# Weight sums of the first feed-forward unit: the second adding DMA writes to DRAM, onto a plain copy of the block, and the transfers of this stage keep program order

## The chip, the cores and the metric

One core of one Trainium2 chip runs the whole program. The metric is the device time of one execution in microseconds (us). The kernel before takes 1514.77 us, the median of three runs (1513.19 to 1515.32). One further execution was profiled; all rows below are from it.

## The reference

The kernel computes one transformer block on 528 tokens (16 meta tokens and 512 real ones) with a model width of 1024, all in float32: a gated feed-forward unit of width 2816, a mixer with retention and sparse attention, a second feed-forward unit, and norms between them.

```python
def swiglu(u, w_gate, w_up, w_down):
    return (jax.nn.silu(u @ w_gate) * (u @ w_up)) @ w_down
...
h = h + 0.5 * swiglu(rmsnorm(h, ffn1_norm[l]), ffn1_w_gate[l], ffn1_w_up[l], ffn1_w_down[l])
h = h + hybrid_mixer(rmsnorm(h, mix_norm[l]), ...)
h = h + 0.5 * swiglu(rmsnorm(h, ffn2_norm[l]), ffn2_w_gate[l], ffn2_w_up[l], ffn2_w_down[l])
y = rmsnorm(h, final_norm)
```

The change concerns the first `swiglu` alone.

## The kernel before

**Products.** Each float32 operand is split in a high and a low part (`whi`, `wlo`: ScalarE makes the high one, VectorE the low one), and each product is made of three TensorE passes. To save passes, blocks of 2 x 2 are multiplied with seven products in place of eight, which needs sums and differences of blocks on both sides.

**Gate and up.** The 22 column tiles of the hidden layer are taken in pairs; `f` is the first tile of a pair. A pair takes eight steps on TensorE: four for the gate weights (one "seven", lines 448 to 515), then four for the up weights. The four steps hold 2, 2, 2 and 1 of the seven products. One load brings the weights of a seven, 1024 KB, into one of two buffers `raw`. It is issued by SyncE (SP) in line 133. A load is written in the program four steps ahead of the step that uses it, and the sums of weights for a seven (lines 466, 467, 471 on VectorE) are made while the seven before it is at its second and third step. So VectorE reads a load about two steps before TensorE does, and a buffer is free once VectorE has made the low part of its last quarter.

**The spill.** For the 16 tiles from `F0` = 4 to `F1` = 20, eight pairs counted by `k`, the product silu(gate) * up is not multiplied with the down weights at once. It goes to DRAM (`hx1`) with four sums of its token and tile halves: `spill1` makes the sums on VectorE (lines 915 to 917, tile `ts`) and stores them with three DMAs from GpSimd (POOL), lines 918 and 920.

**The weight sums.** The down weights of the same 16 tiles are needed in sums of blocks too. For each `k` there are four blocks of 128 x 512 (256 KB). Line 929 loads the left and the right block of the first row, the right one twice (`first`, `total`, `other`). An adding DMA of POOL adds the right block of the second row onto `total` (line 931). `sums1` makes two differences on VectorE (lines 936 and 937), stores three results to DRAM (`wx1`, lines 938 to 940, by SP), lets a second adding DMA add the left block of the second row onto `first` in SBUF (line 941, POOL), and stores that sum from POOL (line 942).

**Where this is called.** `s1.extra` is a list of functions. One is taken off in the first step of each seven and one in the fourth. For pair `k` these are `nothing`, `nothing`, `sums1` (first step of the up seven) and `bring_next` (fourth step of the up seven), which calls `bring1` for `k` + 1. `bring1(0)` is called ahead of the pipeline.

**Order.** TensorE, VectorE and ScalarE run in the order in which the code is written. The DMA issues on SP and POOL are placed by a scheduler, which may move one ahead of another that was written before it, except where `keep_in_program_order` pins it. Before, only the DMAs of the products after this stage are pinned (`in_order`). A queue issues in order: an issue that waits holds back all that stand behind it on the same engine. Where the code of `R` and `wq` speaks of buffers: `first` alternates between `wq` and one of the two `R`, `total` takes the other `R`, and `other` has the single `ssum2`. All R and ssum2 tiles are named `hraw` in the rows.

Of the kernel before, what the change touches and what calls it, by code (L numbers as in the profile page):

```python
# [11 lines left out]
F32 = mybir.dt.float32  # L12
F32R = mybir.dt.float32r
AF = mybir.ActivationFunctionType
ALU = mybir.AluOpType
# [3 lines left out]
P = 128  # L19
D = 1024  # L20
KD = D // P
S = 512
# [59 lines left out]
def kernel(ctx: ExitStack, tc: tile.TileContext, x, meta, g1, wg1, wu1, wd1, gm,  # L82
                      w_in, w_ro, w_ao, w_mo, g2, wg2, wu2, wd2, gf, rope, decay, causal, out):
    nc = tc.nc
# [173 lines left out]
    R = cpool.tile([P, T], F32, name="R", tag="R", bufs=2)  # L258
    late = {}
    ssum2 = cpool.tile([P, T], F32, name="ssum2", tag="ssum2")  # L260
# [11 lines left out]
    hx1 = dpool.tile([8, P, 8, TH], F32, name="hx1")  # L272
# [71 lines left out]
    class Sevens:  # L344
# [103 lines left out]
        def seven(self, src_w, f, take, soon=False):  # L448

            d, th = {}, self.th  # L450
            c1, c2 = slice(0, P), slice(P, 2 * P)

            def product(ps, w, j, name, first):
                mm3([(ps[:, :th], slice(0, th))], [t[:, j : j + 4, :] for t in w], self.moving(name), 4, first, True, not first)

            def copy(name, ps):
                d[name] = self.rooms.tile([P, th], F32, tag=name, name=name, bufs=2)
                nc.scalar.activation(d[name], ps[:, :th], AF.Copy)

            def pre1():  # L460
                d["raw"] = load_w(src_w[:, f * P : (f + 2) * P], KD, 2 * P)

            def pre2():
                raw = d["raw"]
                s = d["s"] = self.wsum()[:, : 16 * P].rearrange("p (a k c) -> p a k c", a=4, k=4)
                nc.vector.tensor_tensor(s[:, 1], raw[:, :4, c2], raw[:, 4:, c2], ALU.add)
                nc.vector.tensor_tensor(s[:, 0], s[:, 1], raw[:, :4, c1], ALU.subtract)

            def pre3():
                raw, s = d["raw"], d["s"]  # L470
                nc.vector.tensor_tensor(s[:, 2], raw[:, :4, c1], raw[:, :4, c2], ALU.subtract)
                self.sum4 = lambda: nc.vector.tensor_tensor(s[:, 3], raw[:, 4:, c1], s[:, 0], ALU.subtract)

            def run1(w, lower):
                d["X"], d["Z"], d["Y"] = (self.bank(f"psq{c}") for c in "XZY")
                product(d["X"], w, 0, "B11", True)
                copy("p1", d["X"])
                lower()
                product(d["Z"], w, 4, "B21", True)
                take(0, d["Z"], d["p1"])  # L480
                self.catch_up()
                if self.extra:
                    self.extra.pop(0)()

            def run2(w, lower):
                product(d["X"], w, 0, "T2", False)
                copy("u2", d["X"])
                lower()
                product(d["Y"], w, 4, "T1", True)
                copy("p5", d["Y"])  # L490

            def run3(w, lower):
                product(d["X"], w, 0, "T3", False)
                take(3, d["X"], d["p5"])
                lower()
                self.next_sum4()
                product(d["Y"], w, 4, "B22", False)
                take(1, d["Y"], d["u2"])

            def run4(w, lower):  # L500
                product(d["X"], w, 0, "T4", False)
                if not soon:
                    lower()
                take(2, d["X"], None)
                if soon:
                    lower()
                if self.extra:
                    self.extra.pop(0)()

            return [(pre1, lambda: d["raw"][:, :, c1], run1),  # L510
                    (pre2, lambda: d["s"][:, 0:2].rearrange("p a k c -> p (a k) c"), run2),
                    (pre3, lambda: d["s"][:, 2:4].rearrange("p a k c -> p (a k) c"), run3),
                    (lambda: None, lambda: d["raw"][:, 4:, c2], run4)]

# [55 lines left out]
    if True:  # L570
# [335 lines left out]
        def one_row(tag):  # L906

            return cpool.tile([P, T], F32, tag=tag, name="hraw", bufs=2 if tag == "R" else 1)

        def spill1(f, u):  # L910

            k = (f - F0) // 2
            all4 = hidp.tile([P, 2, TX], F32, tag=turn(room_tags), name="ts")[:, :, :T].rearrange("p a (b t) -> p a b t", b=2)
            ts = [all4[:, i // 2, i % 2] for i in range(4)]
            nc.vector.tensor_tensor(all4[:, :, 0], u[:, 1::2], u[:, 0:2], ALU.subtract)
            nc.vector.tensor_tensor(ts[1], ts[0], u[:, 3], ALU.subtract)
            nc.vector.tensor_tensor(ts[3], u[:, 2], ts[1], ALU.add)
            nc.gpsimd.dma_start(hx1[0:4, :, k, :].rearrange("o p t -> p o t"), u)
            for i in range(2):
                nc.gpsimd.dma_start(hx1[4 + 2 * i : 6 + 2 * i, :, k, :].rearrange("o p t -> p o t"), all4[:, i])  # L920

        blocks = {}

        def bring1(k):

            blocks["now"] = []
            for tag, (half, cs) in zip((("wq", "R")[k % 2], "R", "ssum2"), ((0, C1), (0, C2), (0, C2))):
                t = hidp.tile([P, S], F32, tag="wq", name="wq") if tag == "wq" else one_row(tag)[:, :S]
                nc.sync.dma_start(t, wrows1[half][:, k, cs])
                blocks["now"].append(t)  # L930
            nc.gpsimd.dma_start(blocks["now"][1], wrows1[1][:, k, C2], accum_op=ALU.add)

        def sums1(k):

            first, total, other = blocks["now"]
            nc.vector.tensor_tensor(other, first, other, ALU.subtract)
            nc.vector.tensor_tensor(first, first, total, ALU.subtract)
            nc.sync.dma_start(wx1[1, :, k, :], other)
            nc.sync.dma_start(wx1[0, :, k, :], total)
            nc.sync.dma_start(wx1[2, :, k, :], first)  # L940
            nc.gpsimd.dma_start(first, wrows1[1][:, k, C1], accum_op=ALU.add)
            nc.gpsimd.dma_start(wx1[3, :, k, :], first)

        def nothing(k):
            pass

        def bring_next(k):

            if k < 7:
                bring1(k + 1)  # L950

        s1.spill = {f: (lambda u, f=f: s1.behind.append(lambda: spill1(f, u))) for f in range(F0, F1, 2)}
        s1.extra = [lambda k=k, do=do: do(k) for k in range(8) for do in (nothing, nothing, sums1, bring_next)]
        unit, ahead, streams = {}, [4], {}

        def in_order(*args):

            tc.keep_in_program_order(nc.sync.dma_start(*args))

        def load_row(src, nk, n):  # L960

# [281 lines left out]
        class Values:  # L1243
# [63 lines left out]
            def take(self, bank_, r):  # L1307
                v = self.by_columns(r)
                nc.vector.tensor_tensor(v, self.by_tokens(self.d[bank_ + "w"]), v, ALU.add)
# [78 lines left out]
        steps += units[1].steps(units[2], rope_beside(ret_k, slice(0, T))) + [gate_step(OFF_GR + P, 1)]  # L1388
        steps += units[2].steps(None, rope_beside(ret_q, REAL))
        n_dense = len(steps)  # L1390
        bring1(0)
        pipe = steps_through(steps, ahead)
        with tc.manual_schedule(engines=BUSY):
            pr = s1.spare("l", "pr")
# [1299 lines left out]
```

## Time and profile before

| | |
|---|---|
| median of three runs | 1514.77 us |
| the profiled execution: its own time | 1514.32 us |
| its span, first to last instruction | 1512.4 us |
| TensorE busy | 99% of the span |
| VectorE busy | 78% of the span |
| the stage of the eight spilled pairs | about 85 to 266 us of the span |
| mean DMA rate over the span | 171 GB/s |

The profile has one row for each group, wait or instruction. Rows of engines are named PE (TensorE), PEld (its weight loads), DVE (VectorE), ACT (ScalarE), POOL (GpSimd), and SPq for the DMA issues of SyncE. The row of a DMA shows when it was issued; "to landing" is the time from there until its data had arrived. Idle time stands in square brackets behind an instruction, with what ended it.

### The profile page before, as it was taken

The page shows a single profiled execution, that of the slowest core. Times are in us where ns is not written, and L with a number is a line of the kernel's source. Part 1 is how long each engine was busy: PE and PEld are TensorE (multiplying, and loading weights), DVE is VectorE, ACT ScalarE, POOL GpSimd, SP SyncE. Part 2 cuts the span into 40 slices and gives each one's busy share as a digit, 9 for nine tenths or more (in the row PEclk, how much of TensorE's full clock was granted, in tenths as well). Part 3 has the DMA queues.
Part 4 walks back from the last instruction along what each step waited for, and adds up shares of the span by engine and source line. Part 5 has one row for each costly group of instructions (what it writes and reads, how often), then busy time and mean ns, then how long its engine had stood idle before and what let it go on. Part 6 is the DMA issues. An engine that isn't in the chain of part 4 may idle for free.

```text
span 1512.4 us, 24591 instructions
## 1 busy us (share of the span) xinstructions
PE 1496.7 (99%) x9647; PEld 1351.6 (89%) x9647; DVE 1179.3 (78%) x1820; ACT 752.2 (50%) x1204; POOL 190.1 (13%) x237
## 2 busy tenths in 40 slices
PE   9999999999999999999999999999999999999998
PEld 8999999999988888788898889999888889999986
DVE  4998898789787767677968676777575788999877
ACT  5655455567354444542333455555335345555555
POOL 1011121001111111000000021111002003222101
PEclk9999999999999999999999999999999999999999
DMA  5259887886645435232322485456583223455693
GB/s 183 85 168 269 242 245 238 292 283 199 236 139 177 168 133 170 87 98 87 108 97 85 99 208 164 149 180 204 166 271 112 84 84 124 163 175 174 232 321 136
DMA packets 183235, 258.44 MB, mean 171 GB/s; under 512 B 9360, under 2 KB 120616, under 8 KB 182224
## 3 DMA queue, kind: packets, MB, share of 16 engines
q1 hardware_dynamic: 164784, 207.42, 42.4%
q0 software_dynamic: 15088, 43.63, 10.1%
q10 hardware_dynamic: 3248, 5.84, 1.2%
q8 instruction: 75, 1.23, 0.3%
q14 instruction: 40, 0.33, 0.1%
HBM read 204.40 MB, written 49.82 MB: 168 GB/s over the span
## 4 chain that ended last, share of the span: by engine, by line
PE 88%; DVE 6%; DMA 4%; issue 1%; ACT 0%; DVEq 0%; ACTq 0%
PE psqX L157 8%; PE psrg L157 6%; PE psro L157 6%; PE psvX L1335 4%; PE psqY L157 4%; DMA raw<-in_ffn_w_gate_dram 3%; PE psrk L157 3%; PE psak L157 3%; PE psu L157 3%; PE psrq L157 3%; PE psgate L157 3%; PE psmo L157 3%; PE psga L157 3%; PE psaq L157 3%; PE psat L157 3%; PE psX L1010 2%
## 5 line engine op out<-in xcount | busy, mean ns | idle before, releaser
L292 DVE TENSOR_TENSOR wlo<-raw,whi 128x1024 fp32r<-128x1024 f32 (+2 forms) x205 | 224.3, 1095 | 47.8 <-ACT whi L291 47.0
L291 ACT ACTIVATE whi<-raw 128x1024 fp32r<-128x1024 f32 (+2 forms) x205 | 192.6, 941 | 129.8 <-PE psqZ L157 21.3
L157 PE MATMUL psqX<-th,whi 128*128 128x264 f32 (+1 forms) x432 | 124.5, 288 | 7.2 <-DVE g L538 5.1
L157 PE MATMUL psqX<-tl,whi 128*128 128x264 f32 (+1 forms) x432 | 122.6, 284 | 0.0
L157 PE MATMUL psqX<-th,wlo 128*128 128x264 f32 (+1 forms) x432 | 122.5, 284 | 0.0
L117 ACT ACTIVATE whi<-raw 128x1024 fp32r<-128x1024 f32 (+1 forms) x58 | 60.3, 1043 | 85.9 <-issue 18.4
L118 DVE TENSOR_TENSOR wlo<-raw,whi 128x1024 fp32r<-128x1024 f32 (+1 forms) x58 | 69.9, 1205 | 40.0 <-ACT whi L117 39.9
L291 ACT ACTIVATE whi<-wsum 128x1024 fp32r<-128x1024 f32 x72 | 76.1, 1057 | 38.6 <-issue 12.6
L157 PEld LDWEIGHTS psqX<-th,whi 128*128 128x128 f32 x432 | 82.2, 190 | 9.6 <-DVE g L538 6.1
L292 DVE TENSOR_TENSOR wlo<-wsum,whi 128x1024 fp32r<-128x1024 f32 x72 | 86.4, 1217 | 0.8 <-ACT whi L291 0.7
L157 PEld LDWEIGHTS psqX<-th,wlo 128*128 128x128 f32 x432 | 82.4, 191 | 0.0
L157 PEld LDWEIGHTS psqX<-tl,whi 128*128 128x128 f32 x432 | 82.3, 191 | 0.0
L157 PE MATMUL psro<-vo,whi 128*128 128x512 f32 x256 | 79.3, 391 | 0.0
L157 PEld LDWEIGHTS psro<-vo,whi 128*128 128x128 f32 x256 | 48.1, 188 | 10.5 <-ACT whi L291 0.2
L157 PE MATMUL psrg<-xh,whi 128*128 128x512 f32 x128 | 51.8, 405 | 0.0
L157 PE MATMUL psro<-vo,wlo 128*128 128x512 f32 x128 | 50.3, 393 | 0.0
L157 PE MATMUL psrg<-xh,wlo 128*128 128x512 f32 x128 | 50.0, 391 | 0.0
L157 PE MATMUL psrg<-xl,whi 128*128 128x512 f32 x128 | 50.0, 390 | 0.0
L292 DVE TENSOR_TENSOR wlo<-w,whi 128x1024 fp32r<-128x1024 f32 x30 | 36.5, 1222 | 13.1 <-ACT whi L291 13.1
L2488 POOL TENSOR_TENSOR ts<-g 128x256 f32<-128x256 f32 x16 | 22.3, 1410 | 176.8 <-DVE g L549 96.3
L291 ACT ACTIVATE whi<-w 128x1024 fp32r<-128x1024 f32 x30 | 31.7, 1057 | 20.1 <-PE psvX L1335 10.9
L157 PE MATMUL psqX<-xh,whi 128*128 128x264 f32 (+1 forms) x144 | 41.3, 286 | 0.0
(516 smaller groups left out, 4832.6 us busy)
## 6 DMA issues: line engine op xcount, KB each, us to landing
raw<-in_ffn_w_up_dram SPq DMA_DIRECT2D x22, 1024.0 KB, 5.2
raw<-in_ffn_w_gate_dram SPq DMA_DIRECT2D x21, 1024.0 KB, 7.1
raw<-in_w_in_dram SPq DMA_DIRECT2D x19, 1024.0 KB, 5.1
raw<-in_ffn_w_down_dram SPq DMA_DIRECT2D x34, 512.0 KB, 4.6
raw<-wx SPq DMA_DIRECT2D x32, 512.0 KB, 5.6
raw<-in_w_in_dram SPq DMA_DIRECT2D x31, 512.0 KB, 4.1
w<-in_w_in_dram SPq DMA_DIRECT2D x24, 512.0 KB, 6.6
wq<-in_ffn_w_down_dram SPq DMA_DIRECT2D x36, 256.0 KB, 5.2
```

The lines of the kernel that those rows point to most:

```text
L117: nc.scalar.activation(hi, src, AF.Copy)
L118: eng.tensor_tensor(lo, src, hi.bitcast(F32), ALU.subtract)
L157: nc.tensor.matmul(o, a[:, k, :], b[:, sl], start=first and k == 0 and i == 0, stop=last and k == nk - 1 and i == 2, skip_group_check=onto)
L291: nc.scalar.activation(hi, src, AF.Copy)
L292: return lambda: nc.vector.tensor_tensor(lo, src, hi.bitcast(F32), ALU.subtract)
L1010: nc.tensor.matmul(pss[c], a[:, k, c * P : (c + 1) * P], m[:, k, :], start=first and k == 0 and i == 0, stop=last and k == 1 and i == 2, s ...
L1335: nc.tensor.matmul(d[bank_][t], a, b[:, k, :], start=not onto and j + k + m == 0, stop=j + k == 3 and m == 2, skip_group_check=onto)
L2488: nc.gpsimd.tensor_tensor(ts[:, i], a, b, ALU.subtract)
```

## The change

The second adding DMA no longer adds onto `first` in SBUF. The left block of the second row of weights is copied from DRAM to DRAM, into its place in `wx1`, ahead of time; the adding DMA then adds `first` from SBUF onto that place, and the store that followed goes. `first` always has the buffer `wq`, is loaded by POOL and not by SP, and is brought in the first step of the next gate seven. `bring_next` moves from the fourth step of the up seven to the third. All DMAs of the weight sums and of the spill are pinned to program order. `spill1` runs in `catch_up`, ahead of the function taken from `s1.extra`, so the three stores to `hx1` stand on POOL ahead of the load of `first`. The order of instructions on TensorE and ScalarE is the same as before; on VectorE it is the same too, only that in four of the eight pairs `first` lies in `wq` in place of `hraw`.

```diff
@@ run3 and run4 of a seven
                 product(d["Y"], w, 4, "B22", False)
                 take(1, d["Y"], d["u2"])
+                if self.extra:
+                    self.extra.pop(0)()
...
                 if soon:
                     lower()
-                if self.extra:
-                    self.extra.pop(0)()
@@ spill1
-            nc.gpsimd.dma_start(hx1[0:4, :, k, :].rearrange("o p t -> p o t"), u)
+            pool_order(hx1[0:4, :, k, :].rearrange("o p t -> p o t"), u)
             for i in range(2):
-                nc.gpsimd.dma_start(hx1[4 + 2 * i : 6 + 2 * i, :, k, :].rearrange("o p t -> p o t"), all4[:, i])
+                pool_order(hx1[4 + 2 * i : 6 + 2 * i, :, k, :].rearrange("o p t -> p o t"), all4[:, i])
@@ weight sums
-        def bring1(k):
-
-            blocks["now"] = []
-            for tag, (half, cs) in zip((("wq", "R")[k % 2], "R", "ssum2"), ((0, C1), (0, C2), (0, C2))):
-                t = hidp.tile([P, S], F32, tag="wq", name="wq") if tag == "wq" else one_row(tag)[:, :S]
-                nc.sync.dma_start(t, wrows1[half][:, k, cs])
-                blocks["now"].append(t)
-            nc.gpsimd.dma_start(blocks["now"][1], wrows1[1][:, k, C2], accum_op=ALU.add)
+        def in_order(*args):
+
+            tc.keep_in_program_order(nc.sync.dma_start(*args))
+
+        def pool_order(*args, **how):
+
+            tc.keep_in_program_order(nc.gpsimd.dma_start(*args, **how))
+
+        def bring_two(k):
+
+            total, other = one_row("R")[:, :S], one_row("ssum2")[:, :S]
+            for t in (total, other):
+                in_order(t, wrows1[0][:, k, C2])
+            pool_order(total, wrows1[1][:, k, C2], accum_op=ALU.add)
+            return [total, other]
+
+        def bring_first(k):
+
+            t = hidp.tile([P, S], F32, tag="wq", name="wq")
+            pool_order(t, wrows1[0][:, k, C1])
+            return [t]
 
         def sums1(k):
 
-            first, total, other = blocks["now"]
+            total, other, first = blocks["now"]
             nc.vector.tensor_tensor(other, first, other, ALU.subtract)
             nc.vector.tensor_tensor(first, first, total, ALU.subtract)
-            nc.sync.dma_start(wx1[1, :, k, :], other)
-            nc.sync.dma_start(wx1[0, :, k, :], total)
-            nc.sync.dma_start(wx1[2, :, k, :], first)
-            nc.gpsimd.dma_start(first, wrows1[1][:, k, C1], accum_op=ALU.add)
-            nc.gpsimd.dma_start(wx1[3, :, k, :], first)
+            for i, t in ((1, other), (0, total), (2, first)):
+                in_order(wx1[i, :, k, :], t)
+            pool_order(wx1[3, :, k, :], first, accum_op=ALU.add)
+
+        def bring_next(k):
+
+            blocks["now"] = bring_two(k + 1)
+            pool_order(wx1[3, :, k + 1, :], wrows1[1][:, k + 1, C1])
+
+        def next_first(k):
+
+            if k:
+                blocks["now"] += bring_first(k)
...
-        s1.extra = [lambda k=k, do=do: do(k) for k in range(8) for do in (nothing, nothing, sums1, bring_next)]
+        s1.extra = [lambda k=k, do=do: do(k) for k in range(8) for do in (next_first, nothing, sums1, bring_next)][:31]
@@ ahead of the pipeline
-        bring1(0)
+        blocks["now"] = bring_two(0) + bring_first(0)
+        pool_order(wx1[3, :, 0, :], wrows1[1][:, 0, C1])
```

The order on SP, before, over one pair and a half. `raw` is a load of gate or up weights, `wx_92` is `wx1`; L929 loads blocks of the down weights, L938 to L940 store `other`, `total` and `first`.

```order
L940 DMA wx_92<-wq 128x512
L929 DMA hraw<-in_ffn_w_down_dram 128x512 x2
L133 DMA raw<-in_ffn_w_up_dram 128x8x256
L939 DMA wx_92<-hraw 128x512
L929 DMA wq<-in_ffn_w_down_dram 128x512
L133 DMA raw<-in_ffn_w_gate_dram 128x8x256
L938 DMA wx_92<-hraw 128x512
L940 DMA wx_92<-hraw 128x512
L929 DMA hraw<-in_ffn_w_down_dram 128x512 x2
L133 DMA raw<-in_ffn_w_up_dram 128x8x256
```

The same place on SP in the changed program, where all pinned DMAs have the line of their helper, L926.

```order
L926 DMA wx_92<-wq 128x512
L926 DMA hraw<-in_ffn_w_down_dram 128x512 x2
L133 DMA raw<-in_ffn_w_up_dram 128x8x256
L133 DMA raw<-in_ffn_w_gate_dram 128x8x256
L926 DMA wx_92<-hraw 128x512 x2
L926 DMA wx_92<-wq 128x512
L926 DMA hraw<-in_ffn_w_down_dram 128x512 x2
L133 DMA raw<-in_ffn_w_up_dram 128x8x256
```

Between the load of the up weights and that of the next gate weights stood the store of `total`, which waits for its adding DMA, and the load of `first`. Both have left this place: the store stands behind the gate load, with the two others, and the load is POOL's.

The order on POOL before, over one pair and a half: the second adding DMA (L941), the first one (L931), the store of the sum (L942), the three stores of the spill (L918, L920).

```order
L941 DMA wq<-in_ffn_w_down_dram 128x512
L931 DMA hraw<-in_ffn_w_down_dram 128x512
L942 DMA wx_92<-wq 128x512
L918 DMA hx_91<-g 128x4x264
L920 DMA hx_91<-ts 128x2x264 x2
L941 DMA hraw<-in_ffn_w_down_dram 128x512
L931 DMA hraw<-in_ffn_w_down_dram 128x512
L942 DMA wx_92<-hraw 128x512
```

The same place on POOL in the changed program, where the helper's line is L930.

```order
L930 DMA wx_92<-wq 128x512
L930 DMA hraw<-in_ffn_w_down_dram 128x512
L930 DMA wx_92<-in_ffn_w_down_dram 128x512
L930 DMA hx_91<-g 128x4x264
L930 DMA hx_91<-ts 128x2x264 x2
L930 DMA wq<-in_ffn_w_down_dram 128x512
L930 DMA wx_92<-wq 128x512
L930 DMA hraw<-in_ffn_w_down_dram 128x512
```

The store that waited for the second adding DMA and stood ahead of the spill is gone; a copy from DRAM to DRAM stands there, which waits for no result of this pair. Behind the spill follows the load of `first`, and then the adding DMA onto DRAM, which is the first row.

More of the change, by code (lines that the diff above doesn't have):

```diff
@@ L942, in sums1 @@
-            nc.gpsimd.dma_start(wx1[3, :, k, :], first)
+            for i, t in ((1, other), (0, total), (2, first)):
[7 more added lines that the diff above has]
+                blocks["now"] += bring_first(k)
         def nothing(k):
             pass
-        def bring_next(k):
-            if k < 7:
-                bring1(k + 1)
@@ L952 @@
         s1.spill = {f: (lambda u, f=f: s1.behind.append(lambda: spill1(f, u))) for f in range(F0, F1, 2)}
-        s1.extra = [lambda k=k, do=do: do(k) for k in range(8) for do in (nothing, nothing, sums1, bring_next)]
+        s1.extra = [lambda k=k, do=do: do(k) for k in range(8) for do in (next_first, nothing, sums1, bring_next)][:31]
         unit, ahead, streams = {}, [4], {}
-        def in_order(*args):
-            tc.keep_in_program_order(nc.sync.dma_start(*args))
         def load_row(src, nk, n):
```

## The prediction

> **What bounds the kernel now.** TensorE is the bound nearly everywhere, so I first ask how much it loses at all. The page's head gives the span and the busy time.
>
> ```profile
> span 1512.4 us, 24591 instructions
> PE 1496.7 (99%) x9647; PEld 1351.6 (89%) x9647; DVE 1179.3 (78%) x1820; ACT 752.2 (50%) x1204; POOL 190.1 (13%) x237
> ```
>
> TensorE is idle for only 15.7 us. The second view, busy time by stretches of the span, shows where; the numbers are the stretch, its length, busy PE, PEld, DVE, ACT and POOL, the granted clock, the DMA share and GB/s.
>
> ```profile
> 30.00:120.00 90.00, 90.00 (x748) 89.83 (x747) 79.34 (x119) 49.90 (x79) 6.82 (x8) 1.00 0.48 143
> 120.00:180.00 60.00, 56.32 (x458) 55.16 (x456) 52.12 (x78) 29.71 (x47) 13.68 (x18) 1.00 0.89 261
> 180.00:190.00 10.00, 9.87 (x69) 9.87 (x70) 8.05 (x13) 5.45 (x10) 0.00 (x0) 0.83 0.65 206
> 190.00:210.00 20.00, 20.00 (x169) 20.00 (x167) 17.50 (x26) 10.90 (x18) 4.56 (x6) 1.00 0.91 265
> 210.00:250.00 40.00, 36.69 (x300) 36.04 (x299) 35.74 (x53) 20.14 (x31) 9.17 (x12) 1.00 0.85 244
> 250.00:300.00 50.00, 50.00 (x415) 49.91 (x414) 40.82 (x58) 28.33 (x44) 3.65 (x5) 1.00 0.81 270
> ```
>
> The stage of the change loses 3.68 + 0.13 + 3.31 = 7.1 us of TensorE, and once the clock falls: 0.83 over 10 us is another 1.7 us. Ahead of it and behind it nothing is lost. So **8.8 us is all that this stage can give**, 0.6% of the span. The third view, the waits from 90 to 280 us, says who ends the idle time (total, times, longest).
>
> ```profile
> DVE wsum L466 <- DMA raw<-in_ffn_w_gate_dram: 10.3, 6, 3.1
> DVE wsum L466 <- DMA raw<-in_ffn_w_up_dram: 2.1, 1, 2.1
> PE psqX L157 <- DVE g L538: 5.1, 5, 2.1
> PE psqX L157 <- DVE g L524: 2.0, 1, 2.0
> ```
>
> TensorE waits for VectorE, and VectorE for a load: 10.3 us for gate weights, 2.1 us for up weights. Those 12.4 us cost 8.8 us of TensorE, 0.71 us for each. The gate loads come too late. Why, is read from the timeline of the pair at 100 to 124 us: SP (with the last up load, seven pairs on), then POOL, then VectorE.
>
> ```profile
> 102.29 0.38 SPq L133 DMA_DIRECT2D raw<-in_ffn_w_up_dram  x1
> 111.74 0.33 SPq L939 DMA_DIRECT2D wx<-hraw  x1
> 113.51 0.33 SPq L929 DMA_DIRECT2D wq<-in_ffn_w_down_dram  x1
> 113.94 1.06 SPq L133 DMA_DIRECT2D raw<-in_ffn_w_gate_dram  x1
> ...
> 255.76 0.38 SPq L133 DMA_DIRECT2D raw<-in_ffn_w_up_dram  x1
> ```
>
> ```profile
> 103.40 0.90 POOL L941 DMA_DIRECT2D wq<-in_ffn_w_down_dram  x1 [61.68 <-DVE g L538]
> 105.32 0.86 POOL L931 DMA_DIRECT2D hraw<-in_ffn_w_down_dram  x1 [1.02 <-DMA hraw<-in_ffn_w_down_dram]
> 110.76 0.58 POOL L942 DMA_DIRECT2D wx<-wq  x1 [4.58 <-DMA wq<-in_ffn_w_down_dram]
> 111.33 0.81 POOL L918 DMA_DIRECT2D hx<-g  x1
> 112.12 1.43 POOL L920 DMA_DIRECT2D hx<-ts  x2
> ```
>
> ```profile
> 106.48 1.25 DVE L549 TENSOR_TENSOR g<-g,st 128x1056 f32<-128x1056 f32 x1
> 110.33 0.43 DVE L917 TENSOR_TENSOR ts<-g,ts 128x264 f32<-128x264 f32 x1
> 110.68 0.69 DVE L466 TENSOR_TENSOR wsum<-raw 128x512 f32<-128x512 f32 x1
> 112.01 0.68 DVE L292 TENSOR_TENSOR wlo<-raw,whi 128x512 fp32r<-128x512 f32 x1
> 119.85 0.69 DVE L937 TENSOR_TENSOR hraw<-hraw 128x512 f32<-128x512 f32 x1
> 122.16 0.69 DVE L466 TENSOR_TENSOR wsum<-raw 128x512 f32<-128x512 f32 x1 [1.61 <-DMA raw<-in_ffn_w_gate_dram]
> ```
>
> The gate load's buffer is free at 112.69, when the last low part is made. VectorE asks for the data at 120.54. That leaves 7.85 us. SP issues at 113.94, since the store L939 (waiting for the adding DMA) and the load of `first` stand ahead; the load takes 8.2 us and is 1.6 us late. Two causes, then: 1.25 us of queueing at most, and a slow transfer. The next rows show why it is slow: first the busy share of the DMA engines in four stretches of this pair, then issue to landing from 100 to 266 us.
>
> ```profile
> 102.00:104.00 2.00, 2.00 (x19) 2.00 (x19) 1.95 (x4) 0.75 (x1) 0.60 (x1) 1.00 0.68 138
> 104.00:111.00 7.00, 7.00 (x61) 7.00 (x60) 6.93 (x11) 3.82 (x6) 1.39 (x3) 1.00 1.02 260
> 111.00:112.00 1.00, 1.00 (x11) 1.00 (x10) 0.96 (x2) 0.48 (x2) 1.00 (x2) 1.00 0.14 47
> 112.00:122.00 10.00, 10.00 (x85) 10.00 (x84) 7.79 (x12) 6.01 (x10) 1.54 (x3) 1.00 1.00 326
> ```
>
> ```profile
> raw<-in_ffn_w_up_dram SPq DMA_DIRECT2D x8, 1024.0 KB, 5.6
> raw<-in_ffn_w_gate_dram SPq DMA_DIRECT2D x7, 1024.0 KB, 8.2
> wx<-hraw SPq DMA_DIRECT2D x18, 256.0 KB, 2.9
> hraw<-in_ffn_w_down_dram SPq DMA_DIRECT2D x17, 256.0 KB, 3.9
> hx<-g POOLq DMA_DIRECT2D x8, 528.0 KB, 4.5
> hx<-ts POOLq DMA_DIRECT2D x16, 264.0 KB, 5.7
> wq<-in_ffn_w_down_dram POOLq DMA_DIRECT2D x4, 256.0 KB, 7.1
> wx<-wq POOLq DMA_DIRECT2D x4, 256.0 KB, 2.5
> ```
>
> From 112 to 122 the DMA engines are full (1.00, 326 GB/s). Just before, at 111, they stand nearly empty (0.14): POOL waited 4.58 us for its adding DMA, and with it waited the three spill stores, 1056 KB, whose first data had been ready since 107.73. Then the spill, the store L942, the load of `first` and the gate load fall into one stretch.
>
> **The change, part by part.** *Gate load on SP.* It now stands right behind the up load, so it is issued when its buffer is free: 1.25 us earlier here. Nothing waits longer for it. *Spill stores on POOL.* Line 918 needs only the product that is ready at 107.73, and POOL is then through with the adding DMA of `total` (105.32) and the copy (about 106.2 to 107). So 528 KB leave at 107.8 in place of 111.33, and the two others at 110.76, when L917 ends, in place of 112.12. *Other transfers.* The store of `total` (L939) moves behind the gate load, to 119.9; the store L942 goes. Out of the gate load's stretch fall 528 KB + 256 KB + 256 KB, 1.06 MB, or 3.3 us at 326 GB/s. The gate load lands at about 122.1 - 3.3 = 118.8 in place of 122.1, before 120.54, with 1.7 us to spare. **The 10.3 us of gate waits go: 10.3 x 0.71 = 7.3 us.** VectorE has no instruction more, so nothing new is late there.
>
> *Up load.* What left the gate stretch arrives here. The store of `total` now lies ahead of the up load on SP (256 KB, 0.8 us at 326 GB/s), and the adding DMA L941 no longer waits for the store of `first`, so it lands more within the up load. There is room: 0.32 x 2 = 0.6 us unused from 102 to 104 and 0.86 us from 111 to 112. The up load came in time at 110.68, where L466 shows no wait. The copy and the early spill store are issued behind it, from 106 on. I let the one up wait of 2.1 us stay, 1.5 us of TensorE.
>
> *The pinned loads of `total` and `other`* are issued at the same place as before, right behind the stores; `bring_next` comes one step earlier only in the program. Their buffers are the same, so the cost is nothing; what would show otherwise is a wait of SP ahead of them.
>
> *The load of `first`* now follows the spill on POOL: issued at about 110.76 + 1.43 = 112.2, needed before L936 at about 119.1. From below, the store L942 (2.5 us) has it there at 114.7; from above, POOL's adding load from the same weights (7.1 us) at 119.3, 0.2 us late. Without the reading of a destination I take 5.7, as for `hx<-ts`: 117.9. Cover gone, each us costs VectorE a us and TensorE 0.71.
>
> *Adding onto DRAM, and the copy.* No row shows either. For the adding DMA the bounds are a plain store (2.5 us) and an adding load plus another reading of DRAM (7.1 + 3.9 = 11.0 us); I take 7.1, the nearest row, since it too reads and writes 256 KB once each. The copy lies between 2.5 and 3.9 + 2.5 = 6.4 us; I take 3.9. Neither is waited for by an engine: `first`'s buffer must be free by 112.2, and issued at about 103.4 the sum has 8.8 us for that. Against a load, a store and an adding DMA before, the number of 256 KB transfers is unchanged at nine per pair, and they may even cost less than before.
>
> The TensorE clock: the fall to 0.83 stands right behind an idle time of 2.0 us, and the sum counts it as lost through waits. The Trainium skill ("TensorE: Matmul & The Clock Gate", Part 1) puts the fall to half speed behind an idle window of about 3.4 us; the longest wait here is 2.1 us, so by that rule these waits would not explain it, and 1.7 us of the gain would be uncertain.
>
> **Sum.** The profiled execution took 1514.3 us (span 1512.4 and 1.9 around it), 0.5 us below the median of the runs, 1514.77. 1514.3 - 8.8 + 1.5 = **1507.0 us**.
>
> **Rivals.** *The engines are full, and the wait only moves to the up load.* For it: shares of 0.89 and 0.91 over long stretches, the up load's thin margin, 1.02 from 104 to 111. Against it: the hole at 111. With waits of 1.5 to 2 us at each of eight up loads VectorE waits 12 to 16 us again; at 0.71 that is 8.5 to 11.4 us, so 1514 to 1517. The Trainium skill ("DMA: Bandwidth & Descriptors", Issuing engines are not separate DMA queues) speaks for this: issuing from another engine only saves issue time, since all transfers share the same 16 engines. The row at 111 agrees only in part, because there the order left the engines idle. Chance 0.14.
>
> *`first` is late.* POOL issues it 7 us before it is needed. If it lands 9 us after its issue, VectorE waits 2 us in seven pairs, 14 x 0.71 = 10 us, about 1515; if 8 us, about 1511. Against it: half of the spill is gone from the engines by then. Chance 0.10.
>
> *Slower: adding onto DRAM holds the DMA engines.* A pair moves 2 x 1024 + 9 x 256 + 1056 = 5408 KB, 5.54 MB. At 261 GB/s for a share of 0.89, full engines need 18.9 us for that. A pair now lasts (255.76 - 102.29) / 7 = 21.9 us; without loss, (153.5 - 8.8) / 7 = 20.7. If one 256 KB sum onto DRAM occupies the engines 1.8 us longer than the sum in SBUF, the gain begins to go; above 3.0 us a pair is longer than now. At 4.0 us longer each of eight pairs loses 1.0 us against now: 1522. Chance 0.13.
>
> *The gate loads issue no earlier* because something else holds SP. The order on SP excludes it, but for the wait on the buffer itself.
>
> **How the numbers follow.** The forecast, waits mostly gone, has 0.63 and reaches from 1504.5 (all 8.8 us and run to run noise) to 1511. A change within 0.2%, 3 us, can't be told from none in this kernel. Adding the first two rivals up to 1517 leaves out only the slower case and a little: **1504.5 to 1517**. Faster 0.66 (a part of the late `first` is still faster), the same 0.20, slower 0.14.
>
> **What would show it.** Right: gate loads land in 5 to 6.5 us and VectorE's waits on them vanish; POOL issues the store of `g` within 1 us of L549's end; TensorE's idle time from 120 to 250 us falls below 2 us; no clock below 1.00 at 180 us. Wrong: waits of L466 on up loads, or of L936 on `wq`, or a landing of the adding DMA onto DRAM above 10 us with a share near 1.00 throughout.

## The result, and the profile after

The changed kernel takes 1504.84 us, the median of six runs (1503.93 to 1505.61); the kernel before, on the same chip, 1515.05 (1512.02 to 1516.67). The ratio is 0.9935 with a 95% interval of 0.9922 to 0.9948: 0.65% faster, inside the range and 2.2 us below the predicted 1507.0. The execution that was profiled took 1505.61 us.

The page's head, the changed kernel:

```profile
span 1503.8 us, 24586 instructions
PE 1493.6 (99%) x9647; PEld 1349.3 (90%) x9647; DVE 1179.7 (78%) x1820; ACT 752.2 (50%) x1204; POOL 194.3 (13%) x245
```

The span is 8.6 us shorter. TensorE's idle time fell from 15.7 to 1503.8 - 1493.6 = 10.2 us, and its busy time by 3.1 us, for the same 9647 matmuls; by the estimate of the prediction 1.7 us of that are the clock. Where the idle time went, the view by stretches shows (columns as before):

```profile
120.00:180.00 60.00, 59.04 (x489) 58.73 (x488) 55.98 (x83) 32.23 (x51) 15.36 (x21) 1.00 0.90 273
180.00:190.00 10.00, 10.00 (x85) 10.00 (x84) 9.46 (x14) 5.85 (x11) 1.12 (x2) 1.00 0.77 214
190.00:210.00 20.00, 19.57 (x163) 19.36 (x162) 18.40 (x28) 10.39 (x18) 5.15 (x8) 1.00 0.89 265
210.00:250.00 40.00, 40.00 (x335) 40.00 (x334) 38.08 (x57) 22.12 (x36) 9.96 (x14) 1.00 0.90 273
```

The stage now loses 0.96 + 0.43 = 1.4 us in place of 7.1, and the clock stays at 1.00 from 180 to 190. VectorE's waits for loads and TensorE's waits for VectorE in the changed kernel, from 90 to 280 us (total, times, longest):

```profile
DVE wsum L466 <- DMA raw<-in_ffn_w_gate_dram: 2.0, 2, 1.9
DVE wsum L466 <- DMA raw<-in_ffn_w_up_dram: 1.1, 2, 0.8
PE psqX L157 <- DVE g L538: 1.0, 1, 1.0
PE psqX L157 <- DVE g L524: 0.4, 1, 0.4
```

VectorE waits 3.1 us for weights, where it waited 12.4. No row has VectorE waiting for `first`. Why the loads are in time, the timelines of the changed kernel show: SP, then POOL, in the pair that was shown of before.

```profile
102.64 0.38 SPq L133 DMA_DIRECT2D raw<-in_ffn_w_up_dram  x1
113.07 0.38 SPq L133 DMA_DIRECT2D raw<-in_ffn_w_gate_dram  x1
```

```profile
100.98 0.90 POOL L930 DMA_DIRECT2D wx<-wq  x1 [57.17 <-DVE wq L950]
106.37 0.87 POOL L930 DMA_DIRECT2D hraw<-in_ffn_w_down_dram  x1 [4.49 <-DMA hraw<-in_ffn_w_down_dram]
106.92 0.87 POOL L930 DMA_DIRECT2D wx<-in_ffn_w_down_dram  x1
108.38 0.82 POOL L930 DMA_DIRECT2D hx<-g  x1 [0.59 <-DVE g L549]
110.94 1.43 POOL L930 DMA_DIRECT2D hx<-ts  x2 [1.74 <-DVE ts L916]
112.37 0.55 POOL L930 DMA_DIRECT2D wq<-in_ffn_w_down_dram  x1
```

Between the up load and the gate load SP issues nothing. POOL issues the store of `g` at 108.38 (before: 111.33), right after the 0.59 us that it waits for the data itself, and the two stores of `ts` at 110.94 (before: 112.12). The busy share of the DMA engines in the same four stretches:

```profile
102.00:104.00 2.00, 2.00 (x19) 2.00 (x18) 1.95 (x5) 1.10 (x2) 0.00 (x0) 1.00 1.06 234
104.00:111.00 7.00, 7.00 (x61) 7.00 (x60) 6.93 (x10) 3.82 (x6) 2.30 (x4) 1.00 1.02 282
111.00:112.00 1.00, 1.00 (x10) 1.00 (x10) 0.97 (x3) 0.13 (x1) 1.00 (x2) 1.00 1.08 387
112.00:122.00 10.00, 10.00 (x85) 10.00 (x84) 9.22 (x14) 6.02 (x11) 1.73 (x3) 1.00 0.76 265
```

The hole at 111 (0.14) is filled, and the gate load's stretch from 112 to 122 has fallen from 1.00 to 0.76. From issue to landing, 100 to 266 us:

```profile
raw<-in_ffn_w_up_dram SPq DMA_DIRECT2D x8, 1024.0 KB, 8.1
raw<-in_ffn_w_gate_dram SPq DMA_DIRECT2D x7, 1024.0 KB, 6.8
wx<-wq POOLq DMA_DIRECT2D x8, 256.0 KB, 6.1
wx<-in_ffn_w_down_dram POOLq DMA_DIRECT2D x7, 256.0 KB, 5.6
wq<-in_ffn_w_down_dram POOLq DMA_DIRECT2D x7, 256.0 KB, 4.7
```

The gate load takes 6.8 us in place of 8.2, the up load 8.1 in place of 5.6: traffic has moved from the one to the other, as the prediction had it, and the up load is late by only 1.1 us in all.

### The profile page after: what moved, and what is told of

It reads as the page before. It is cut to its first block, busy times and chain, and to the rows that moved or that the text cites. A ratio compares the mean times of both kernels' runs of the same rounds, so it can differ in the third digit from the quotient of the medians.

```text
span 1503.8 us, 24586 instructions
## 1 busy us (share of the span) xinstructions
PE 1493.6 (99%) x9647; PEld 1349.3 (90%) x9647; DVE 1179.7 (78%) x1820; ACT 752.2 (50%) x1204; POOL 194.3 (13%) x245
## 4 chain that ended last, share of the span: by engine, by line
PE 90%; DVE 5%; DMA 3%; issue 1%; ACT 0%; ACTq 0%; DVEq 0%
PE psqX L157 10%; PE psrg L157 6%; PE psro L157 6%; PE psqY L157 5%; PE psvX L1347 4%; PE psrk L157 3%; PE psak L157 3%; PE psu L157 3%; PE psrq L157 3%; PE psgate L157 3%; PE psmo L157 3%; PE psga L157 3%; PE psaq L157 3%; PE psat L157 3%; PE psqZ L157 2%; PE psX L1022 2%
## 5 line engine op out<-in xcount | busy, mean ns | idle before, releaser
L291 ACT ACTIVATE whi<-w 128x1024 fp32r<-128x1024 f32 x30 | 31.7, 1057 | 20.1 <-PE psvX L1347 10.9
L157 PE MATMUL psqY<-th,whi 128*128 128x264 f32 (+1 forms) x144 | 40.8, 283 | 0.0
```

The source lines that it names most:

```text
L157: nc.tensor.matmul(o, a[:, k, :], b[:, sl], start=first and k == 0 and i == 0, stop=last and k == nk - 1 and i == 2, skip_group_check=onto)
L291: nc.scalar.activation(hi, src, AF.Copy)
```

## The experiments

Three theories of the gain. **A**: the spill stores no longer stand behind a waiting store on POOL, so 0.5 to 1 MB leave the gate load's stretch. **B**: on SP the gate load is issued earlier, with nothing ahead of it. **C**: adding onto DRAM itself. The diffs are shortened: helper functions and the handling of the first and the last pair are left out. The table gives each kernel's ratio to the kernel before and VectorE's waits for gate loads, up loads and `first` from 90 to 280 us in its profile. Each ratio is against runs of the kernel before on the same chip and in the same group; the medians of before lie between 1514.05 and 1516.47.

| kernel | median us | ratio (95%) | gate | up | `first` |
|---|---|---|---|---|---|
| before | 1515.05 | 1 | 10.3 | 2.1 | 0 |
| changed | 1504.84 | 0.9935 (0.9922 to 0.9948) | 2.0 | 1.1 | 0 |
| sp_order_alone | 1523.55 | 1.0056 (1.0036 to 1.0075) | 0.7 | 0.7 | 11.7 |
| pool_order_alone | 1503.45 | 0.9936 (0.9913 to 0.9959) | 1.3 | 3.5 | 0 |
| both_orders_sbuf | 1510.73 | 0.9975 (0.9966 to 0.9985) | 0 | 1.5 | 9.7 |
| sp_not_pinned | 1510.49 | 0.9971 (0.9958 to 0.9983) | 0 | 11.1 | 0 |
| pool_order_alone_again | 1503.98 | 0.9936 (0.9923 to 0.9950) | 0.6 | 0 | 0 |
| changed_again | 1503.94 | 0.9932 (0.9920 to 0.9945) | 2.1 | 1.5 | 0 |
| copies_all_ahead | 1503.99 | 0.9937 (0.9923 to 0.9951) | 0 | 3.6 | 0 |
| first_ahead_of_spill | 1504.01 | 0.9937 (0.9920 to 0.9954) | 0.4 | 1.3 | 0 |
| one_copy_more | 1504.84 | 0.9924 (0.9910 to 0.9939) | 1.1 | 0.9 | 0.5 |
| three_copies_more | 1509.56 | 0.9958 (0.9941 to 0.9974) | 6.1 | 0 | 3.8 |
| store_between | 1514.65 | 0.9989 (0.9977 to 1.0002) | 5.8 | 7.5 | 0 |
| first_behind_gate | 1509.94 | 0.9958 (0.9943 to 0.9972) | 9.8 | 1.1 | 0 |

### SP's order alone

The changed kernel, but the sum is again made in SBUF and stored from POOL ahead of the spill. No copies.

```diff
@@ sums1
-            pool_order(wx1[3, :, k, :], first, accum_op=ALU.add)
+            pool_order(first, wrows1[1][:, k, C1], accum_op=ALU.add)
+            blocks["left"] = lambda: pool_order(wx1[3, :, k, :], first)
@@ bring_next
             blocks["now"] = bring_two(k + 1)
-            pool_order(wx1[3, :, k + 1, :], wrows1[1][:, k + 1, C1])
+            blocks.pop("left")()
```

> The order on SP as after the change (gate load right behind the up load, the three stores behind it), the sum onto first made in SBUF and stored from POOL ahead of the spill stores, as before the change; first is loaded by POOL behind the spill. Theory A (the gate load was late because 1 MB of other transfers lay in its stretch; each part of the change counts by what it takes out of there): the store of total leaves the stretch (0.8 us) and the load is issued up to 1.25 us earlier, against gate waits of 1.7 us on average: 1506 to 1510 us. Theory B (the place of the gate load on SP, behind a waiting store, is all): 1504 to 1506 us. Theory C (adding onto DRAM is what gives the time): 1513 to 1516 us.

Slower than before, which no theory had. The gate waits are nearly gone (0.7 us), but two new waits came. The two of this kernel:

```profile
DVE hraw L949 <- DMA wq<-in_ffn_w_down_dram: 11.7, 6, 3.3
DVE g L538 <- DMA hx<-g: 7.7, 2, 4.5
```

`first` has one buffer here and is loaded by POOL at 113.72, behind the store and the spill; VectorE waits for it in six pairs. And VectorE waits twice for a late spill store whose buffer it needs. So POOL's order was not merely undone but made worse: the kernel before had given `first` two buffers and loaded it on SP a pair ahead. No forecast had these waits, so the run decides between none of the theories. That the gate waits are nearly gone does not speak for B either: VectorE takes `first` (L949) shortly ahead of the gate load (L466), so a wait for `first` gives the gate load the same time more; in the pair shown, 1.45 us.

### POOL's order alone

The kernel before, with POOL's DMAs of this stage pinned. The store of the sum is kept in `blocks["left"]`, and `store_left` calls it behind the spill.

```diff
@@ sums1
-            nc.gpsimd.dma_start(wx1[3, :, k, :], first)
+            blocks["left"] = lambda: pool_order(wx1[3, :, k, :], first)
@@ the list of functions
-        s1.extra = [lambda k=k, do=do: do(k) for k in range(8) for do in (nothing, nothing, sums1, bring_next)]
+        s1.extra = [lambda k=k, do=do: do(k) for k in range(8) for do in (store_left, nothing, sums1, bring_next)]
```

> The program before the change, but POOL stores the sum of L942 behind the three spill stores and not ahead of them; SP as before. Theory A: 528 KB leave the gate load's stretch, 1.65 us at 326 GB/s, against gate waits of 1.7 us on average: 1506 to 1510 us, gate waits of VectorE below 4 us in total. Theory B: 1513 to 1516 us. Theory C: 1513 to 1516 us.

> The kernel before, with only POOL's store of the left sum moved behind the three spill stores, a second time and in more rounds, beside the changed kernel on the same chip. Theory A (the place of that one store on POOL makes the whole gain; the adding onto DRAM, the copies and the order on SP give nothing beyond it): 1503 to 1506 us, the same as the changed kernel within 0.2%. Rival B (it still has up waits that the changed kernel lacks, as the profiled run of 1509.2 us showed): 1507 to 1510 us, between the two.

1503.45 and 1503.98 us: the whole gain, with the sum in SBUF, a store of it, and no copy. Theory C falls, since the changed kernel, in the same group as the second, took 1503.94. The profiled run of the first took 1509.2 us, with one up wait of 3.5 us; none of the eight other runs of this kernel took over 1506.3. POOL, then SP, of pool_order_alone_again:

```profile
108.09 0.81 POOL L916 DMA_DIRECT2D hx<-g  x1 [1.27 <-DVE g L549]
110.65 1.46 POOL L916 DMA_DIRECT2D hx<-ts  x2 [1.75 <-DVE ts L924]
112.10 0.56 POOL L916 DMA_DIRECT2D wx<-wq  x1
```

```profile
111.79 0.33 SPq L947 DMA_DIRECT2D wx<-hraw  x1
112.78 0.38 SPq L133 DMA_DIRECT2D raw<-in_ffn_w_gate_dram  x1
117.43 0.33 SPq L937 DMA_DIRECT2D wq<-in_ffn_w_down_dram  x1
```

But SP's rows show what the expectation had missed. SP was not pinned, and the scheduler put the load of `first`, whose buffer now comes free later, *behind* the gate load (before: 113.51, then the gate load at 113.94). So this kernel has POOL's order and part of SP's, and does not tell A from B. The last experiment makes SP's part alone.

### Both orders, the sum in SBUF

The changed kernel, the sum in SBUF, its store behind the spill.

```diff
@@ sums1
-            pool_order(wx1[3, :, k, :], first, accum_op=ALU.add)
+            pool_order(first, wrows1[1][:, k, C1], accum_op=ALU.add)
+            blocks["left"] = lambda: pool_order(wx1[3, :, k, :], first)
@@ next_first
             if k:
+                blocks.pop("left")()
                 blocks["now"] += bring_first(k)
```

> Both orders as after the change, but the sum onto first made in SBUF and stored by POOL behind the spill; the load of first waits for that store. Theory A: 1504 to 1507 us if first is in time; the load of first now comes about 2.5 us later than after the change, so waits of VectorE for it of 0 to 1 us in each of seven pairs may cost up to 5 us more. Theory B: as sp_order_alone. Theory C: 1513 to 1516 us.

No gate wait is left, but `first` is late. POOL of this kernel:

```profile
111.34 0.55 POOL L930 DMA_DIRECT2D wx<-wq  x1
116.12 0.55 POOL L930 DMA_DIRECT2D wq<-in_ffn_w_down_dram  x1 [4.23 <-DMA wx<-wq]
```

The load of `first` waits 4.23 us until the store has read its only buffer, and VectorE waits 9.7 us for it. That is 5.9 us more time than the changed kernel, where the load goes at 112.37. So this is what adding onto DRAM is good for here: it ends the use of `wq` early enough for a single buffer. Where `first` has two buffers, as in the kernel of POOL's order, the same time is reached without it.

### SP not pinned

The changed kernel, with SP's loads and stores of the weight sums left to the scheduler.

```diff
@@ bring_two
-                in_order(t, wrows1[0][:, k, C2])
+                nc.sync.dma_start(t, wrows1[0][:, k, C2])
@@ sums1
-                in_order(wx1[i, :, k, :], t)
+                nc.sync.dma_start(wx1[i, :, k, :], t)
```

> The changed program, but the stores and loads on SP are not pinned: the store of total, waiting for its adding DMA, stands ahead of the gate load again. Theory A: the gate load is issued up to 1.25 us later and shares its stretch with 256 KB more, 2 us in all, of which 1.7 us are spare: 1504.5 to 1507 us. Theory B: 1512 to 1516 us. Theory C: 1504 to 1506 us.

The forecasts by B (1512 to 1516) and A (1504.5 to 1507) lie on either side. The run does not test what it was meant to: the store of `total` stands ahead of the gate load again, but it goes at 108.02 and does not hold up the gate load, which goes at 113.27, when its buffer is free. The time is lost elsewhere. Waits, landing and POOL of this kernel:

```profile
DVE wsum L466 <- DMA raw<-in_ffn_w_up_dram: 11.1, 7, 3.2
```

```profile
raw<-in_ffn_w_up_dram SPq DMA_DIRECT2D x8, 1024.0 KB, 10.0
raw<-in_ffn_w_gate_dram SPq DMA_DIRECT2D x7, 1024.0 KB, 5.7
```

```profile
100.03 0.90 POOL L930 DMA_DIRECT2D wx<-wq  x1 [56.74 <-DVE wq L950]
100.61 1.22 POOL L930 DMA_DIRECT2D hraw<-in_ffn_w_down_dram  x1
101.16 1.22 POOL L930 DMA_DIRECT2D wx<-in_ffn_w_down_dram  x1
```

The wait moved to the up load, as the first rival of the prediction had it. The scheduler loads `total` a pair ahead, so POOL finds it there and issues both adding DMAs and the copy within 1.2 us, just ahead of the up load at 101.69. In the changed kernel POOL waits 4.49 us, until 106.37, ahead of two of the three, so that only one of the three goes out just ahead of the up load, which is issued at 102.64. I read the difference in the up loads (10.0 us to landing against 8.1) as the work of that wait, which then does good where a wait on POOL did harm in the kernel before; no run changes this wait alone.

### The changed kernel and three near it

Again the changed kernel; the same with all eight copies issued ahead of the pipeline; the same with the load of `first` ahead of the spill stores.

```diff
@@ copies_all_ahead: bring_next, and ahead of the pipeline
-            pool_order(wx1[3, :, k + 1, :], wrows1[1][:, k + 1, C1])
...
-        pool_order(wx1[3, :, 0, :], wrows1[1][:, 0, C1])
+        for k in range(8):
+            pool_order(wx1[3, :, k, :], wrows1[1][:, k, C1])
@@ first_ahead_of_spill: bring_next; next_first does nothing
+            blocks["now"] += bring_first(k + 1)
```

> The changed kernel again, as the measure for the others of this group: 1504 to 1506 us by every theory.

> The changed kernel, but all eight copies of the left blocks are issued ahead of the pipeline, where the DMA engines have room (share 0.48 from 30 to 120 us), and none in the stage of the spilled pairs. Theory A (the gain comes from traffic taken out of the gate load's stretch; what is left to lose is in the 1.4 us of TensorE idle time from 120 to 250 us): each pair moves 256 KB less in the stage, the waits on up loads (1.1 us) and gate loads (2.0 us) shrink, and the time is 0 to 1.5 us below the changed kernel's 1504.8, so 1503.3 to 1505. Rival (the copies lie where they cost something, and taking 0.8 us of DMA per pair away gives more): 1500 to 1503 us. Rival (eight copies at about 40 us hold the loads of the mixer there, which the changed kernel does not): 1506 to 1510 us, with waits on loads ahead of 85 us.

> The changed kernel, but the load of first is written with the loads of total and other, ahead of the spill stores on POOL. Its buffer is free only when the adding DMA onto DRAM has landed. Theory A (what counts is that the spill leaves POOL before the gate load): the adding DMA is issued at about 101 us and lands at about 107, so POOL waits with the load of first until 107 to 108, the spill store of g follows within 1 to 2 us of L549's end, and the time is within 3 us of the changed kernel: 1504 to 1508. Rival (every wait ahead of the spill on POOL costs what the store of the sum cost in the kernel before): POOL waits 3 us or more for the adding DMA, the spill leaves at 110 or later, gate waits come back, and the time is 1510 to 1516 us.

1503.94, 1503.99 and 1504.01 us: no difference. 256 KB less in each pair buy nothing (the gate waits go, and the up waits rise to 3.6 us), so the changed kernel is not bound by the amount. And that the stores stand ahead of the load of `first` does not matter: POOL, with the load ahead of them, was held by it for 1.0 us at most in any pair; in the kernel before, the store of the sum held it for 4.58 to 6.10 us. With the run of POOL's order, four kernels stand at 1503.9 to 1504.0, and none of those tried is faster.

### One copy more, three copies more

```diff
@@ bring_next, n = 1 or 3; spare is a tensor in DRAM that nothing reads
+            for i in range(n):
+                pool_order(spare[i, :, k + 1, :], wrows1[1][:, k + 1, C1])
```

> The changed kernel with one further copy of 256 KB from DRAM to DRAM in each pair from the second on, into a tensor that nothing reads, issued behind the copy of the left block. Theory D (the DMA engines are near full but not the bound: a pair's transfers need some 18.9 us of full engines, and a pair lasts 20.6 us): a copy needs 0.8 to 1.6 us of the engines, which fits; 1504 to 1508 us, with waits of VectorE on loads of 3 to 6 us in place of 3.1. Rival (the engines are the bound, any 256 KB more costs its full time in each of seven pairs): 1510 to 1515 us.

> The same with three further copies in each pair. Theory D: 2.4 to 4.8 us of engine time more, above the 1.7 us that are free, so 0.7 to 3.1 us lost in each of seven pairs: 1509 to 1526 us, with DMA shares of 0.95 and more and waits on up and gate loads of 7 us or more. Rival (the order of transfers decides alone, the engines have room): 1504 to 1507 us.

One copy is free (ratio 0.9924, the changed kernel 0.9932). Three cost 4.7 us against one, by the medians of the same group, and 5.2 by the ratios (0.9958 against 0.9924): the low end of what the budget of a pair gave, 0.7 to 3.1 us in each of seven pairs. Stretch and waits with three copies more:

```profile
120.00:180.00 60.00, 58.61 (x483) 58.17 (x482) 55.31 (x82) 32.14 (x51) 20.10 (x30) 1.00 0.97 303
```

```profile
DVE wsum L467 <- DMA raw<-in_ffn_w_gate_dram: 6.1, 7, 1.9
DVE hraw L950 <- DMA wq<-in_ffn_w_down_dram: 3.8, 3, 1.9
```

At a share of 0.97 the gate loads and `first` are late again, though the up loads are not. So the changed kernel has room for one transfer of 256 KB more per pair and not for three; two were not tried. The page numbers lines from one further on in this kernel (its L467 is L466 elsewhere).

### The store between the spill stores

The kernel of POOL's order, but the store of the sum stands behind the spill store of `g` only, and ahead of the two of `ts`.

```diff
@@ spill1
             pool_order(hx1[0:4, :, k, :].rearrange("o p t -> p o t"), u)
+            store_left(k)
             for i in range(2):
```

> The kernel before with POOL's store of the left sum moved behind the first spill store only, the one of g (528 KB), so ahead of the two stores of ts. Theory A (what counts is that the 528 KB whose data are ready at about 107 do not stand behind a waiting store): the store of g leaves at 107 to 108, those of ts at most 1 us later than when the store of the sum stands behind all three, and the time is 1503.5 to 1506.5, like that one. Rival E (the whole spill has to be ahead of that store; the gate load must not share its stretch with ts either): half the gain, 1508 to 1512 us, with gate waits of 4 us or more.

No gain that can be told (1514.65, interval 0.9977 to 1.0002), where A had 1503.5 to 1506.5 and its rival E 1508 to 1512: both missed. SP of this kernel:

```profile
111.66 0.33 SPq L948 DMA_DIRECT2D wx<-hraw  x1
114.99 0.33 SPq L938 DMA_DIRECT2D wq<-in_ffn_w_down_dram  x1
115.42 0.38 SPq L133 DMA_DIRECT2D raw<-in_ffn_w_gate_dram  x1
```

The 528 KB of `g` did leave early, at 107.90. But the scheduler had the load of `first` ahead of the gate load again; it waits on SP for the store of the sum, and the gate load goes at 115.42, 1.5 us later than in the kernel before. The gate waits fell to 5.8 us all the same, but three up loads became late, 7.5 us in all; they are issued at 122.92, 167.56 and 233.51, and VectorE has them 10.2 to 11.5 us later. In this kernel the early store of `g` bought nothing. I read it as a gain in the gate loads that a loss on SP and in the up loads cancels; the run does not part the two, and why these three up loads are slow stays open.

### The load of `first` behind the gate load, POOL as before

The kernel before, with the load of `first` written ahead of the stores of `sums1` and pinned behind the gate load. POOL's order is that of before, and SP's order in this stage that of the run of POOL's order: the combination that the runs above lack.

```diff
@@ load_w, from the first call of sums1 on
+        if pinned and nk == KD and n == 256:
+            tc.keep_in_program_order(move)
@@ sums1
+            pinned[:] = [k] * (k < 7)
+            if k < 7:
+                blocks["first"] = bring_first(k + 1)
```

> The kernel before, with POOL's order untouched (the store of the sum still stands ahead of the spill and waits there), and on SP only the load of first moved from ahead of the gate load to behind it. The run that moved POOL's store had this on SP as well, so it has not told the two apart. Theory B (the place of the load of first on SP makes the gain: the gate load is issued as soon as its buffer is free, and 256 KB less lie ahead of it): gate waits of 2 us or less, 1503.5 to 1506.5 us. Theory A (the spill held behind POOL's waiting store makes it): the gate load gains 1 to 1.5 us of issue and 0.8 us of transfer but shares its stretch with the spill as before; gate waits of 3 us or more remain and the time is 1508 to 1513 us. Both needed in part: 1506.5 to 1508.

1509.94 us, in the middle of A's 1508 to 1513: by the ratio 0.42% of the 0.64 that the run of POOL's order gives, by the medians 5.5 us of 10.1. Its stretches at 111 and 112, and its wait:

```profile
111.00:112.00 1.00, 1.00 (x11) 1.00 (x10) 0.96 (x2) 0.31 (x2) 1.00 (x2) 1.00 0.26 74
112.00:122.00 10.00, 10.00 (x86) 10.00 (x85) 9.00 (x14) 6.01 (x11) 1.54 (x3) 1.00 0.97 328
```

```profile
DVE wsum L469 <- DMA raw<-in_ffn_w_gate_dram: 9.8, 7, 2.1
```

The gate load is issued at 112.88, 1.06 us earlier than before, but the hole (0.26) and the full stretch behind it (0.97, 328 GB/s) are still there, since the spill still waits on POOL until 111.33. VectorE waits 9.8 us for gate loads, nearly as long as before, but in seven waits of 2.1 us at most. They cost TensorE less: from 90 to 280 us it is idle 5.1 us (before: 7.1) and loses nothing to the clock (before: 1.7). With the spill stores moved ahead of that store as well (pool_order_alone_again), 0.6 us of waits are left and another 0.22% of the time goes, 3.3 us. The intervals of the two ratios just overlap (0.9943 to 0.9950), but the runs of these two do not (1507.03 to 1511.45, and 1503.47 to 1506.26); of pool_order_alone, one run in four, 1509.2, lies among the slower ones. So SP's place alone gives about two thirds of the gain, and the rest comes with POOL's order. One difference besides is not parted: here the load of `first` goes at 113.61, right behind the gate load, and there at 117.43, when the store of the sum has left its buffer, so that its 256 KB too leave most of the gate load's stretch.

## Why the prediction was right, point by point

- **The bound.** "8.8 us is all that this stage can give": 8.6 us were measured between the spans of the two profiled executions, 10.2 between the medians, so for the medians it was no bound: it was read from one execution. The forecast of 1507.0 stands beside 1505.61 of the profiled execution: the stage loses 1.4 us, as against 1.5 in the sum, so the 1.4 us that are left over lie in TensorE's busy time (3.1 us less, of which the clock is 1.7). No run shows a cause for that part; executions of the changed kernel lie 1.7 us apart, those of the kernel before 4.7.
- **Gate waits go.** 10.3 us to 2.0, not to nothing. Of the two causes that the prediction named, the earlier issue alone does not do it: first_behind_gate keeps 9.8 us of waits, while pool_order_alone_again has both and keeps 0.6. That the lighter stretch alone would not do it either is not shown.
- **The size of the traffic.** Taken: a gate load that needs 6.1 us (112.7 to 118.8). Measured: 6.8, so not within the 5 to 6.5 us that were to show it. It is issued at 113.07 and would by the median land at 119.9, 0.9 us ahead of L466 at 120.81, and not 1.7. The other signs came: in that pair the store of `g` goes 0.3 us behind the end of L549 (108.08), TensorE is idle for 1.4 us from 120 to 250 us, and the clock at 180 is 1.00.
- **The up wait stays: wrong, and small.** Taken 2.1 us; it is 1.1. The up load takes 8.1 us in place of 5.6 and is in time all the same, but for two waits of 0.8 us at most. That the stage's loss agrees with the sum is half luck: the rest of the gate waits takes the place of the up waits that went.
- **0.71 us of TensorE for one of VectorE** is not a constant. After, 1.4 / 3.1 = 0.45; in first_behind_gate 5.1 / 10.9 = 0.47; in sp_not_pinned 7.5 us of idle TensorE from 90 to 250 us over 11.1 give 0.68. I read it so: VectorE is idle for a part of each pair and makes up for short waits there.
- **The load of `first`.** Taken 5.7 us, measured 4.7. Issued at 112.37 it is there at 117.1, and VectorE wants it at 119.48. The rival "late `first`" was real nearby: in both_orders_sbuf and sp_order_alone, where the store of the sum holds its buffer or stands ahead of it, it costs 9.7 and 11.7 us of waits. The rival's times (1515, 1511) were counted from 1505.5, without the up wait that the forecast kept; from 1507.0 each would be 1.5 us more.
- **Adding onto DRAM**: taken 7.1, measured 6.1 us. **The copy**: taken 3.9, measured 5.6, within its bounds. The rival "holds the engines" is out: from 120 to 180 us changed_again moves 276 GB/s at a share of 0.92, pool_order_alone_again with its sums in SBUF 273 at 0.92, and one copy more is free.
- **The clock.** The 1.7 us that were counted as lost through waits came back with them: no stretch shown after is below 1.00.
- **What stays open**: what A alone would give with SP's order as before. Only store_between comes near to it, and there SP's place got worse.

## What to carry to other kernels

A DMA that waits at the head of a queue holds all transfers behind it (here 1056 KB of spill stores, behind a store that waited 4.58 us); when it lets them go, they meet the next big load. So look at the DMA share in the microseconds *ahead* of a late load: in this kernel a hole there, followed by a full stretch, came from order and not from volume. Moving one store on POOL, and with it one load on SP, was worth as much as the new scheme of transfers, and the load alone about two thirds of it. After every move look at the order of all queues again, since a scheduler may have answered on another one, and ask of a freed wait which load its transfers will meet next.

## What the runs showed of the hardware

**The clock falls after some idle times and not after others of like length.** In the kernel before, 2.05 us of idle TensorE were followed by 0.83 over 10 us:

```profile
180.13 0.39 PE L157 MATMUL psqX<-th,whi 128*128 128x264 f32 x1 [2.05 <-DVE g L524]
```

Two longer ones, each with its instruction from the timeline and its stretch: first store_between,

```profile
137.45 0.39 PE L157 MATMUL psqX<-th,whi 128*128 128x264 f32 x1 [2.99 <-DVE g L524]
```

```profile
120.00:180.00 60.00, 55.48 (x457) 54.84 (x455) 50.79 (x75) 29.73 (x47) 13.80 (x18) 1.00 0.86 255
```

then the profiled run of pool_order_alone:

```profile
238.44 0.59 PE L157 MATMUL psqX<-th,whi 128*128 128x264 f32 x1 [3.43 <-DVE g L524]
```

```profile
210.00:250.00 40.00, 36.57 (x281) 36.36 (x281) 31.85 (x48) 19.13 (x31) 6.61 (x9) 0.91 0.75 229
```

After 2.99 us the clock stayed at 1.00. After 3.43 us it fell to a mean of 0.91 over 40 us, 3.6 us, so that one late load cost twice its wait. The Trainium skill ("TensorE: Matmul & The Clock Gate", Part 1) has the clock fall after an idle window of about 3.4 us. The 3.43 and the 2.99 us agree with that; the 2.05 us do not. Nor is it the only one. Of the eight idle times of 1.9 to 3.0 us that the profiles of these kernels have between 84 and 270 us, four were followed by a fall (1.91, 2.05, 2.42 and 2.61 us) and four were not (1.90, 2.13, 2.42 and 2.99); the three longer ones (3.43, 4.73 and 4.78) all were. What makes a short one count was not tried.

**Adding onto DRAM took about as long as adding onto SBUF**: 6.1 us from issue to landing for 256 KB, against 7.1 and 5.5 us for the two that add onto SBUF tiles (`wq` before, `total` after), each beside the other traffic of its place in the pair. A copy from DRAM to DRAM of the same size took 5.6 us, and POOL's plain load of 256 KB 4.7.
